# Input projection cut into columns of 512, 512, 260 and 260, with the halves of the squares added on GpSimd

## The chip, the cores and the metric

One core of a Trainium2 chip runs the whole kernel. The metric is the device time of one execution in microseconds (us), the median of several runs; lower is better.

## The reference

One layer of a streaming encoder, in fp32, with 2048 tokens of 1024 features and a memory of 256 tokens.

```python
# per layer (DEPTH = 1)
xn = rmsnorm(h, g_mix)
z = einsum('bsd,dc->bsc', xn, w_in)          # q | k | v (512 each), pool input (512), 8 forget logits
q, k = rmsnorm per head of 64
fox = forgetting_attention(q, k, v, f_logit) # causal softmax with cumulated log gates, 8 heads
pool = multiscale_pool(p_in)                 # trailing means over 2, 4, 8, 16 frames, linear map
h = h + concat(fox, pool) @ w_out
mn = rmsnorm(mem, g_mem_kv);  mkv = mn @ w_mem_kv
h = h + attention of rmsnorm(h) over the memory (4 heads of 128) @ w_mem_out
h = h + SwiGLU(rmsnorm(h))                   # 2816 hidden features
```

RMSNorm divides a token by the root of the mean of its squares. The part that concerns us is the first projection, `z`, and the two sums of squares it needs: those of the memory tokens and those of the tokens `x`.

## The kernel before

Every fp32 product is made from three products of split operands. `split` makes a high part (ScalarE casts to fp32r) and a low part (VectorE subtracts), and `mm3` issues high x high, high x low and low x high into the same PSUM bank (lines 65 to 70). So every logical matmul shows as three, on lines 68, 69 and 70.

**Order.** In the first part of the program (the `first` block) the instructions of TensorE, VectorE, ScalarE, GpSimd and the DMA queue of SyncE run exactly in the order in which they are written. An engine that waits holds up all that stands behind it in that order.

**The memory's keys and values.** For each of 8 slices `k` of 128 features, `split_kv(k)` splits the weights into the buffers `qs`, `kh`, `kl` in turn, and 12 matmuls of 512 columns go into four PSUM banks `kv`. Between the slices the loop has other work: squares of the memory tokens are collected (`x_split` with `mpart`), their sums and the reciprocal root are made at `k == 3` (`token_sums`, `token_rstd`), the first 256 tokens of `x` are split and squared at `k == 5` (`x_split(xt, part)`), and the projection's weights are split at `k == 6` and after the loop (`split_w_in`). `mpart` and `part` are the same single buffer, tag `part`.

**Squares and sums.** `x_split` loads tokens in four pieces of [128 features, 2 slices, 256 tokens]. ScalarE squares each; GpSimd adds the pieces 1 to 3 onto the first, so that `part` holds two halves of 256 tokens. `token_sums` adds over the features with TensorE: the squares are the stationary operand and a column of ones the moving one, for each half of the tokens (`j`) and each half of the squares (`c`) one matmul with a single column. `token_rstd` copies the sums out of PSUM with VectorE (line 213) and makes the reciprocal root with two small GpSimd operations (lines 77 and 79).

**The projection.** The 1544 columns of `w_qkvf` (q, k, v and 8 forget logits) are cut into four groups of `ZB = 386`. For each of 16 token tiles of 128 tokens, `project` runs 4 groups x 8 slices x 3 products = 96 matmuls into four PSUM banks `zps` (tag `z`, 4 buffers). In the first tile (`zps0`) the loop over slices is outside, since the weights are still being split; in the others the loop over groups is outside, and group 0 is followed by transposes of earlier heads (`to_heads`, line 402) and, in every second tile, by `token_sums` of the tile pair's squares. `scaled` evicts the four banks with ScalarE (line 350), multiplied by the token's reciprocal root. Then come the head norms (`normed_heads`, `gained_heads`, `head_parts`), and more transposes. The squares of the next block of 256 tokens are made a whole tile before they are summed.

After this stage come the projection of the pool input (`zp`), the pooling, the attention, the memory's attention and the SwiGLU stage, which the change does not touch.

Of the kernel before, what the change touches and what calls it, by code (L numbers as in the profile page):

```python
# [8 lines left out]
F32 = mybir.dt.float32  # L9
F32R = mybir.dt.float32r  # L10
AF = mybir.ActivationFunctionType
ALU = mybir.AluOpType
# [4 lines left out]
P = 128  # L17
S = 2048
D = 1024
KD = D // P  # L20
# [11 lines left out]
EPS = 1e-6  # L32
BIG = 3.0e38
QKVF = 3 * FOXW + H
ZB = QKVF // 4

# [2 lines left out]
def block_kernel(ctx: ExitStack, tc: tile.TileContext, x, xT, memT, cols, rows, w_qkvf, w_p, w_pool, w_out,  # L41
# [4 lines left out]
    act, dve, pool, pe, sp = nc.scalar, nc.vector, nc.gpsimd, nc.tensor, nc.sync  # L46

    def opened(stack, name, bufs=1, **kw):
        return stack.enter_context(tc.tile_pool(name=name, bufs=bufs, reuse_waits="tile", **kw))
# [12 lines left out]
    def sub_hi(lo, src, hi, eng=None):  # L62
        (eng or dve).tensor_tensor(out=lo, in0=src, in1=f(hi), op=ALU.subtract)  # L63

    def mm3(ps, st, mv, first, last, goes_on=False):

        (sh, sl), (mh, ml) = st, mv
        pe.matmul(ps, lhsT=sh, rhs=mh, start=first, stop=False, skip_group_check=goes_on)  # L68
        pe.matmul(ps, lhsT=sh, rhs=ml, start=False, stop=False, skip_group_check=goes_on)  # L69
        pe.matmul(ps, lhsT=sl, rhs=mh, start=False, stop=last, skip_group_check=goes_on)  # L70
# [22 lines left out]
    ones = cst.tile([P, P], F32, name="ones")  # L93
# [8 lines left out]
    def more_constants():  # L102
        dve.tensor_copy(identr[:], ident[:])

        dve.tensor_scalar(out=gqs[:, 0, :], in0=gqf, scalar1=-(DH ** -0.5), scalar2=None, op0=ALU.mult)
        dve.tensor_copy(gqs[:, 1, :], gkf)
        dve.tensor_scalar(out=gqm[:], in0=gq_mem, scalar1=P ** -0.5, scalar2=None, op0=ALU.mult)
    rstd = cst.tile([P, NT], F32, name="rstd")
# [16 lines left out]
    def slab(n, pl=None, dt=F32):  # L125
        n = ("qs", "kh", "kl", "cb")[n]
        return (pl or hpa).tile([P, S], dt, tag=n, name=n, bufs=1)
# [29 lines left out]
    def x_split(tiles, part=None, qs=range(4)):  # L157

        for q in qs:
            n, raw = tiles[q]  # L160
            hi = xp.tile([P, 2, B], F32R, tag="xhi", name="xhi", bufs=8)
            act.copy(hi[:], raw[:])
            if part is not None:
                sq = xp.tile([P, 2, B], F32, tag="xsq", name="xsq", bufs=2)[:] if q else part
                act.activation(sq, raw[:], AF.Square, scale=1.0 / 32.0)
                if q:
                    pool.tensor_tensor(out=part, in0=part, in1=sq, op=ALU.add)
            m, lo = xsl.take(F32R)
            sub_hi(lo[:], raw[:], hi[:])
            xsl.free.append(n)  # L170
            xlow.append(m)
            tiles[q] = hi, lo

    def x_part(tiles, k):
        return tuple(t_[:, k % 2] for t_ in tiles[k // 2])

    def x_parts(tiles):
        return tuple(zip(*(x_part(tiles, k) for k in range(KD))))
# [12 lines left out]
    whi = [None] * KD  # L191
    wlo = [None] * KD
# [4 lines left out]
    with ExitStack() as c0:  # L197
# [4 lines left out]
        def token_sums(part):  # L202

            ssp = tpp.tile([P, 2], F32, tag="ss", name="ss", bufs=1)
            for j in range(2):
                for c in range(2):
                    pe.matmul(ssp[:, j:j + 1], lhsT=part[:, c, j * P:(j + 1) * P], rhs=ones[:, 0:1], start=c == 0,
                              stop=c == 1)
            return ssp

        def token_rstd(ssp, outp):
            ms = xp.tile([P, 2], F32, tag="ms", name="ms", bufs=2)
            dve.tensor_copy(ms[:], ssp[:])
            rsqrt(outp, ms[:])
# [15 lines left out]
        def load_kv(k):  # L230
            wk[k] = w_in_hi(k, F32)[:, :2 * MW]
            sp.dma_start(wk[k], w_mem_kv[k * P:(k + 1) * P, :])

        def split_kv(k):
            t_ = slab(k % 3, dt=F32R)
            hi, lo = t_[:, :2 * MW], t_[:, 2 * MW:]

            w_ = MW if k == 0 else 2 * MW
            for c in range(0, 2 * MW, w_):
                split(hi[:, c:c + w_], lo[:, c:c + w_], wk[k][:, c:c + w_], g_mem_kv[:, k:k + 1])  # L240
            return hi, lo

        def load_w_in(k):

            n, raw = wsl.take(F32) if k < KD - 1 else (None, slab(3))
            w_raw[k] = n, raw[:, :QKVF]
            sp.dma_start(w_raw[k][1], w_qkvf[k * P:(k + 1) * P, :])

        def split_w_in(k):
            n, raw = w_raw[k]  # L250
            whi[k] = w_in_hi(k, F32R)
            wlo[k] = wsl.take(F32R)[1]
            split(whi[k][:], wlo[k][:], raw, g_mix[:, k:k + 1])
            wsl.free.append(n)
# [14 lines left out]
        for k in range(KD):  # L269
            if k == 0:  # L270
                raw = mt[0][1]
                x_split(mt, None, (0,))
            elif k < 4:
                x_split(mt, mpart[:], (k,))
            wh, wl = split_kv(k)
            if k == 0:
                act.activation(mpart[:], raw[:], AF.Square, scale=1.0 / 32.0)
            mh, ml = x_part(mt, k)
            if k == 3:
                token_rstd(token_sums(mpart), mr[:])  # L280
            for m in range(2):
                ms_ = slice(m * P, (m + 1) * P)
                for a in range(2):
                    as_ = slice(a * MW, (a + 1) * MW)
                    mm3(kv[m][a][:], (mh[:, ms_], ml[:, ms_]), (wh[:, as_], wl[:, as_]), k == 0, k == KD - 1)
            if k < 4:
                load_kv(k + 4)
            if k == 1:
                sp.dma_start(rowt[:], rows.partition_broadcast(P))
                load_w_in(0)  # L290
            if k == 3:
                for c in range(1, KD):
                    load_w_in(c)
            if k == 6:
                split_w_in(0)
            if k == 7:
                more_constants()
            if k == 5:
                part = xp.tile([P, 2, B], F32, tag="part", name="part", bufs=1)
                x_split(xt, part[:])  # L300
# [35 lines left out]
        with ExitStack() as c1:  # L336
            zpp = opened(xstack, "zpp", space=PSUM)

            def project(i, j, hs, ls, ns, k_outer=False):
                zps = {n: zpp.tile([P, ZB], F32, tag="z", name="zps", bufs=4) for n in ns}  # L340
                ts = slice(j * P, (j + 1) * P)
                for k, n in ([(k, n) for k in range(KD) for n in ns] if k_outer else [(k, n) for n in ns for k in range(KD)]):
                    sl = slice(n * ZB, (n + 1) * ZB)
                    mm3(zps[n][:], (hs[k][:, ts], ls[k][:, ts]), (whi[k][:, sl], wlo[k][:, sl]), k == 0, k == KD - 1)
                return zps

            def scaled(i, zps):
                z = slab(i % 2)
                for n in zps:
                    act.activation(z[:, n * ZB:(n + 1) * ZB], zps[n][:], AF.Copy, scale=rstd[:, i:i + 1])  # L350
                return z

            ssp = token_sums(part)
            for k in range(2, KD):
                split_w_in(k)
# [145 lines left out]
            for b in range(NB):  # L501
                hs, ls = x_parts(xt)
                for j in range(2):
                    i = 2 * b + j
# [8 lines left out]
                    if i == 0:  # L513
                        zps = zps0
                    else:
                        zps = project(i, j, hs, ls, range(1))
                        if i > 1:
                            to_heads(i - 2, zr, (3,))
                        else:
                            mem_keys()  # L520
                        if j == 0:
                            ssp = token_sums(part)
                        zps.update(project(i, j, hs, ls, range(1, 4)))
                        zr = split_heads(*st_)
                        if j == 0:
                            token_rstd(ssp, rstd[:, i:i + 2])
                    z = scaled(i, zps)
                    if i == NT - 3:
                        rb = stat_rows(stat_bcast(stat_diag(0)))
# [3 lines left out]
                    if j == 0:  # L533
                        if b + 1 < NB:
                            part = xp.tile([P, 2, B], F32, tag="part", name="part", bufs=1)
# [52 lines left out]
    with xstack:  # L588
# [66 lines left out]
        with in_order():  # L655
            mixed, mxs, pos, wop = {}, {}, {}, {}
            for n in range(NB + 3):
                if 0 < n < NB:
                    hs, ls = nxt
# [72 lines left out]
    with ExitStack() as c0:  # L732
# [228 lines left out]
        with in_order(EN.DVE, EN.Activation):  # L961
            sg, vg = all_scores(), all_values()
            lead, more = 0, True
            while True:
                if more and lead < LEAD:
                    n = next(sg, None)
                    more = n is not None
                    lead += more
                else:
                    n = next(vg, None)  # L970
# [136 lines left out]
    with ExitStack() as c0:  # L1107
# [138 lines left out]
        with in_order(EN.SP):  # L1246
# [14 lines left out]
            for n in range(NT + 1):  # L1261
# [6 lines left out]
                i = n + 2 if ahead else n + 1  # L1268
# [16 lines left out]
                i = n - 3  # L1285
# [10 lines left out]
                i = n - 1  # L1296
                if 0 <= i < NT:
                    pmd[i] = softmax(*qtd.pop(i), i >= NT - 3)
                i = n - 2
# [6 lines left out]
                i = n - 4  # L1306
# [314 lines left out]
```

## Time and profile before

| what | us |
|---|---|
| median of 3 runs | 2549.94 (2548.57 to 2550.21) |
| the profiled execution | 2547.98 |
| its span, first to last instruction | 2546.2 |
| TensorE busy in it | 2521.4 |
| VectorE, ScalarE, GpSimd busy | 1702.5, 1247.4, 777.8 |
| start (memory's keys and values), until the first projection | 0 to 34 |
| the input projection | 34 to 333 |

The profile is one execution. Rows of its timeline give the start and the duration of an instruction in us, the engine, the line of the kernel, the operation, out<-in by tile names, the shape, and in brackets the idle time of the engine before it and what ended it. PE is TensorE's matmul side, PEld its weight loads, DVE VectorE, ACT ScalarE, POOL GpSimd, SP SyncE. Matmuls overlap, so the distance between starts says what one costs.

### The profile page before, as it was taken

The page shows a single profiled execution, that of the slowest core. Times are in us where ns is not written, and L with a number is a line of the kernel's source. Part 1 is how long each engine was busy: PE and PEld are TensorE (multiplying, and loading weights), DVE is VectorE, ACT ScalarE, POOL GpSimd, SP SyncE. Part 2 cuts the span into 40 slices and gives each one's busy share as a digit, 9 for nine tenths or more (in the row PEclk, how much of TensorE's full clock was granted, in tenths as well). Part 3 has the DMA queues.
Part 4 walks back from the last instruction along what each step waited for, and adds up shares of the span by engine and source line. Part 5 has one row for each costly group of instructions (what it writes and reads, how often), then busy time and mean ns, then how long its engine had stood idle before and what let it go on. Part 6 is the DMA issues. An engine that isn't in the chain of part 4 may idle for free.

```text
span 2546.2 us, 36944 instructions
## 1 busy us (share of the span) xinstructions
PE 2521.4 (99%) x13155; PEld 2159.2 (85%) x13155; DVE 1702.5 (67%) x3018; ACT 1247.4 (49%) x2376; POOL 777.8 (31%) x1048
## 2 busy tenths in 40 slices
PE   9999999999999989999999999999999999999999
PEld 8999999878888878888878888888888888888887
DVE  7444386579999965545886877756766666665554
ACT  6454452169999945444544333334543333333443
POOL 3243210035554623333343544530001222222000
PEclk9999999999999999999999999999999999999999
DMA  6443375355554232212554554447672323324765
GB/s 250 125 132 109 116 240 157 134 162 144 125 149 133 86 121 75 87 72 87 204 214 168 184 190 162 180 167 274 237 262 101 126 99 109 123 100 173 239 207 204
DMA packets 204202, 396.20 MB, mean 156 GB/s; under 512 B 24305, under 2 KB 99825, under 8 KB 193265
## 3 DMA queue, kind: packets, MB, share of 16 engines
q1 hardware_dynamic: 174800, 297.35, 36.8%
q0 software_dynamic: 29216, 96.49, 9.8%
q8 instruction: 103, 1.69, 0.3%
q14 instruction: 83, 0.67, 0.1%
HBM read 268.85 MB, written 124.91 MB: 155 GB/s over the span
## 4 chain that ended last, share of the span: by engine, by line
PE 59%; DVE 2%; issue 1%; ACT 1%; POOL 0%; DMA 0%; POOLq 0%; DVEq 0%; ACTq 0%
PE bk L70 16%; PE bk L68 16%; PE bk L69 16%; PE mmps L68 3%; PE mmps L70 3%; PE mmps L69 3%; PE tp L985 1%; PE tp L1048 0%; DVE ww L63 0%; PE scps L70 0%; PE scps L69 0%; PE scps L68 0%; PE mops L70 0%; PE mops L69 0%; PE mops L68 0%
## 5 line engine op out<-in xcount | busy, mean ns | idle before, releaser
L63 DVE TENSOR_TENSOR ww<-draw,ww 128x512 fp32r<-128x512 f32 x308 | 204.3, 701 | 156.9 <-ACT ww L186 156.4
L186 ACT CAST ww<-draw 128x512 fp32r<-128x512 f32 x308 | 178.6, 620 | 220.7 <-PE bk L70 176.6
L63 DVE TENSOR_TENSOR ww<-graw,ww 128x512 fp32r<-128x512 f32 x220 | 175.1, 802 | 107.9 <-ACT ww L186 107.7
L69 PE MATMUL bk<-ww,ww 128*128 128x512 f32 x616 | 239.6, 389 | 0.0
L68 PE MATMUL bk<-ww,ww 128*128 128x512 f32 x616 | 239.6, 389 | 0.0
L70 PE MATMUL bk<-ww,ww 128*128 128x512 f32 x616 | 239.6, 389 | 0.0
L186 ACT CAST ww<-graw 128x512 fp32r<-128x512 f32 x220 | 135.8, 621 | 177.3 <-PE bk L70 160.0
L63 DVE TENSOR_TENSOR pl<-tp,ph 128x512 fp32r<-128x512 f32 (+3 forms) x298 | 177.3, 597 | 17.5 <-ACT ph L880 16.7
L68 PE MATMUL zps<-wh,xhi 128*128 128x386 f32 x512 | 175.7, 343 | 0.1
L69 PE MATMUL zps<-wl,xhi 128*128 128x386 f32 x512 | 173.5, 339 | 0.0
L70 PE MATMUL zps<-wh,xl 128*128 128x386 f32 x512 | 173.3, 339 | 0.0
L880 ACT CAST ph<-tp 128x512 fp32r<-128x512 f32 (+3 forms) x298 | 147.6, 514 | 15.1 <-PE tp L55 12.3
L70 PE MATMUL bk<-qs,ww 128*128 128x512 f32 x352 | 137.1, 390 | 1.1 <-DVE ww L63 1.1
L68 PE MATMUL bk<-qs,ww 128*128 128x512 f32 x352 | 137.9, 392 | 0.3 <-ACT s L1433 0.3
L69 PE MATMUL bk<-kh,ww 128*128 128x512 f32 x352 | 137.0, 389 | 0.0
L68 PE MATMUL bk<-kl,ww 128*128 128x512 f32 x352 | 136.9, 389 | 0.0
L69 PE MATMUL bk<-cb,ww 128*128 128x512 f32 x352 | 136.9, 389 | 0.0
L70 PE MATMUL bk<-kl,ww 128*128 128x512 f32 x352 | 136.9, 389 | 0.0
L70 PEld LDWEIGHTS bk<-ww,ww 128*128 128x128 f32 x616 | 115.6, 188 | 24.1
L69 PEld LDWEIGHTS bk<-ww,ww 128*128 128x128 f32 x616 | 115.7, 188 | 24.1
L68 PEld LDWEIGHTS bk<-ww,ww 128*128 128x128 f32 x616 | 115.7, 188 | 23.7
L1514 POOL DMA_DIRECT2D out_dram<-o x32 | 17.2, 540 | 382.6 <-DVE o L1511 376.8
(576 smaller groups left out, 7297.7 us busy)
## 6 DMA issues: line engine op xcount, KB each, us to landing
graw<-in_w_gu_dram SPq DMA_DIRECT2D x44, 1024.0 KB, 5.5
draw<-in_w_down_dram SPq DMA_DIRECT2D x66, 256.0 KB, 4.3
xl<-in_xT_dram SPq DMA_DIRECT2D x64, 256.0 KB, 4.6
qkT<-st SPq DMA_DIRECT2D x64, 256.0 KB, 2.7
wdr<-in_w_down_dram SPq DMA_DIRECT2D x22, 512.0 KB, 4.4
vd<-cb SPq DMA_DIRECT2D x16, 512.0 KB, 3.4
qs<-qkT SPq DMA_DIRECT2D x8, 1024.0 KB, 7.1
kh<-qkT SPq DMA_DIRECT2D x16, 512.0 KB, 9.7
```

The costliest lines, as they stand in the source:

```text
L63: (eng or dve).tensor_tensor(out=lo, in0=src, in1=f(hi), op=ALU.subtract)
L68: pe.matmul(ps, lhsT=sh, rhs=mh, start=first, stop=False, skip_group_check=goes_on)
L69: pe.matmul(ps, lhsT=sh, rhs=ml, start=False, stop=False, skip_group_check=goes_on)
L70: pe.matmul(ps, lhsT=sl, rhs=mh, start=False, stop=last, skip_group_check=goes_on)
L186: act.copy(hi, raw)
L880: act.copy(ph[:, sl], tp[:, sl])
L985: pe.transpose(tp[:, e_], src[:, q + e_], ident[:])
L1514: pool.dma_start(out[rows_, cs], o)
```

## The change

Three things change. The columns are cut at 0, 512, 1024, 1284 and 1544, so that two groups have 512 columns and two have 260; each PSUM tile is a bank of 512 columns of which a group uses its part. After the last piece of squares, GpSimd adds the second half of `part` onto the first (one addition of 128x256), and `token_sums` runs one matmul for each half of the tokens where it ran two. And the memory's sums and reciprocal root move from slice 3 to slice 5 of the memory's loop.

```diff
-ZB = QKVF // 4
+ZCUT = (0, 512, 1024, 1284, QKVF)
...
                 if q:
                     pool.tensor_tensor(out=part, in0=part, in1=sq, op=ALU.add)
+                if q == 3:
+                    pool.tensor_tensor(out=part[:, 0], in0=part[:, 0], in1=part[:, 1], op=ALU.add)
...
             for j in range(2):
-                for c in range(2):
-                    pe.matmul(ssp[:, j:j + 1], lhsT=part[:, c, j * P:(j + 1) * P], rhs=ones[:, 0:1], start=c == 0,
-                              stop=c == 1)
+                pe.matmul(ssp[:, j:j + 1], lhsT=part[:, 0, j * P:(j + 1) * P], rhs=ones[:, 0:1], start=True, stop=True)
             return ssp
...
             mh, ml = x_part(mt, k)
-            if k == 3:
+            if k == 5:
                 token_rstd(token_sums(mpart), mr[:])
...
             def project(i, j, hs, ls, ns, k_outer=False):
-                zps = {n: zpp.tile([P, ZB], F32, tag="z", name="zps", bufs=4) for n in ns}
+                zps = {n: zpp.tile([P, 512], F32, tag="z", name="zps", bufs=4)[:, :ZCUT[n + 1] - ZCUT[n]] for n in ns}
...
-                    sl = slice(n * ZB, (n + 1) * ZB)
-                    mm3(zps[n][:], (hs[k][:, ts], ls[k][:, ts]), (whi[k][:, sl], wlo[k][:, sl]), k == 0, k == KD - 1)
+                    sl = slice(ZCUT[n], ZCUT[n + 1])
+                    mm3(zps[n], (hs[k][:, ts], ls[k][:, ts]), (whi[k][:, sl], wlo[k][:, sl]), k == 0, k == KD - 1)
...
                 for n in zps:
-                    act.activation(z[:, n * ZB:(n + 1) * ZB], zps[n][:], AF.Copy, scale=rstd[:, i:i + 1])
+                    act.activation(z[:, ZCUT[n]:ZCUT[n + 1]], zps[n], AF.Copy, scale=rstd[:, i:i + 1])
```

In the order of the instructions on each engine nothing else moves: behind the projection the two programs issue the same instructions in the same order.

## The prediction

> **What bounds the kernel now.** I read the page first: span, then the busy time of TensorE (PE).
>
> ```profile
> span 2546.2 us, 36944 instructions
> PE 2521.4 (99%) x13155; PEld 2159.2 (85%) x13155; DVE 1702.5 (67%) x3018; ACT 1247.4 (49%) x2376; POOL 777.8 (31%) x1048
> ```
>
> PE is busy for 99% of the span, so what the change takes from PE comes off the end, unless it opens a wait there. Next I read busy time by stage. The input projection of tokens 128 to 2047 lies in 51 to 333 us; columns are length, then busy us and instructions of PE, weight loads, VectorE (DVE), ScalarE (ACT), GpSimd (POOL), then granted clock, DMA share and GB/s.
>
> ```profile
> 51.00:333.00 282.00, 282.00 (x1734) 280.87 (x1733) 125.56 (x140) 134.36 (x232) 101.97 (x68) 1.00 0.39 118
> ```
>
> PE has no idle time there at full clock, and no other engine is busy half of it. In this stage a matmul costs the distance from its start to the next start, not its recorded duration (0.34 us for 386 columns, of which half overlaps the next one). Those distances come from the timeline of PE.
>
> ```profile
> 155.27 0.34 PE L68 MATMUL zps<-wh,xhi 128*128 128x386 f32 x1
> ...
> 163.56 0.34 PE L70 MATMUL zps<-wh,xl 128*128 128x386 f32 x1
> ...
> 335.13 0.28 PE L68 MATMUL zp<-xhi,wph 128*128 128x256 f32 x1
> ...
> 344.49 0.28 PE L70 MATMUL zp<-xhi,wpl 128*128 128x256 f32 x1
> ...
> 950.88 0.28 PE L68 MATMUL scps<-ww,ww 128*128 128x256 f32 x1
> ...
> 952.20 0.28 PE L70 MATMUL scps<-ww,ww 128*128 128x256 f32 x1
> ...
> 2199.84 0.39 PE L68 MATMUL bk<-kl,ww 128*128 128x512 f32 x1
> ...
> 2203.46 0.39 PE L69 MATMUL bk<-s4l,ww 128*128 128x512 f32 x1
> ```
>
> Each pair is the first and last start of an unbroken run. 386 columns: 48 matmuls, 47 steps in 8.29 us, 176.4 ns a step. 256 columns: 80 steps in 9.36 us, 117.0 ns; in another stage 11 steps in 1.32 us, 120 ns. 512 columns: 16 steps in 3.62 us, 226.3 ns.
>
> **Part 1, the cut of the 1544 columns.** A token tile has 96 matmuls (4 groups, 8 slices of features, 3 products). Before, all have 386 columns; after, 48 have 512 and 48 have 260. No row has 260 columns. The line from 256 to 512 has (226.3 - 117.0) / 256 = 0.427 ns a column, so four more columns add 1.7 ns: 118.7 from the lower row, 121.7 from the upper. I take 120. For 512 I take 227, between 226.3 and 228 (an estimate that allows for the slower steps after a switch). Twice in each tile PE returns from 128-column transposes, and the first step is longer:
>
> ```profile
> 163.73 1.14 PE L402 MATMUL tp<-identr,kl 128*128 128x128 f32 x12
> 164.71 0.41 PE L68 MATMUL zps<-wh,xhi 128*128 128x386 f32 x1
> 164.96 0.34 PE L69 MATMUL zps<-wl,xhi 128*128 128x386 f32 x1
> ...
> 1507.12 0.60 PE L1048 MATMUL bk<-ident,h 128*128 128x128 f32 x4
> 1507.47 0.47 PE L68 MATMUL bk<-qs,ww 128*128 128x512 f32 x1
> 1507.79 0.39 PE L69 MATMUL bk<-kh,ww 128*128 128x512 f32 x1
> ```
>
> It takes 0.25 us with 386 columns and 0.32 us with 512; after the change both returns fall on groups of 512. Before: 2 x 0.25 + 94 x 0.1764 = 17.08 us a tile. After: 2 x (0.32 + 23 x 0.227) + 48 x 0.120 = 16.84. That is 0.24 less in each of 15 tiles; the first tile has no return inside it: 96 x 0.1764 - 48 x (0.227 + 0.120) = 0.28. Sum: **-3.9 us**. With 118.7 and 226.3 it is 0.33 a tile, -5.3; with 121.7 and 228 it is 0.11, -1.8.
>
> The Trainium skill, "TensorE: Matmul & The Clock Gate", section "Back-to-back issue gap", gives the warm gap as columns / 2.4 + 2.5 ns. By that rule any cut into four costs the same and this term would be 0. The trace differs: 176.4 ns for 386 where the rule has 163.3, and 226.3 for 512 where it has 215.8, so the fixed part is not one number here. I go by the rows, and keep the rule's outcome as a rival.
>
> ScalarE evicts the four groups with other widths (about as much in sum: 1544 columns either way). Cover: the next tile needs the first bank again at 164.71, as quoted.
>
> ```profile
> 159.35 1.53 ACT L350 ACTIVATE qs<-zps,rstd 128x386 f32<-128x386 f32 x3 [2.47 <-POOL rstd L79]
> ```
>
> The first eviction ends at about 159.35 + 0.51 = 159.9; at 512/386 of its length it would end 0.17 later, against 4.8 us of slack. I cost it at nothing; without that cover it would be 0.17 us a tile, 2.7 in all.
>
> **Part 2, the sums over features.** `token_sums` runs four matmuls with one column, which the trace shows as eight.
>
> ```profile
> 150.06 1.02 PE L207 MATMUL ss<-ones,part 128*128 128x1 f32 x8
> 150.94 0.43 PE L68 MATMUL zps<-wh,xhi 128*128 128x386 f32 x1
> ...
> 135.21 5.75 POOL L167 TENSOR_TENSOR part<-part,xsq 128x512 f32<-128x512 f32 x3
> ```
>
> Eight take 0.88 us, 0.11 each; four go away: 0.44. It happens once for each of 8 blocks of tokens: **-3.5 us** (the call for the memory is in part 3). GpSimd pays with an addition of 128x256: no row has it; between 0.96 us (half of 5.75 / 3) and 1.92. GpSimd's additions end at 140.96, 9.1 us before the sums read them, so the new one is hidden.
>
> **Part 3, the start: the memory's sums move from slice 3 to slice 5.** This is where I expect the money to go. In program order the step on DVE (`ms` from PSUM, L213) now stands behind the low parts of slices 4 and 5 and in front of the four subtractions for the first tokens; on PE it stands behind all matmuls of slice 4. No DMA is issued by the step, and SP's order stays.
>
> ```profile
> 17.86 0.16 DVE L213 COPY ms<-ss 128x2 f32<-128x2 f32 x1 [0.83 <-PE ss L207]
> 19.16 1.28 DVE L182 SCALAR_TENSOR_TENSOR kl<-wh,colt,kl 128x1024 fp32r<-128x1024 f32 x1
> 20.36 4.89 DVE L63 TENSOR_TENSOR xl<-xl,xhi 128x512 fp32r<-128x512 f32 x4
> 25.18 2.32 DVE L182 SCALAR_TENSOR_TENSOR qs<-wh,colt,qs 128x1024 fp32r<-128x1024 f32 x1
> ...
> 19.54 0.63 ACT L165 ACTIVATE part<-xl 128x512 f32<-128x512 f32 x1
> ...
> 18.12 1.21 POOL L77 TENSOR_SCALAR ms<-ms 128x2 f32<-128x2 f32 x1 [2.83 <-DVE ms L213]
> 19.41 1.63 POOL L79 TENSOR_TENSOR mr<-ms,mhalf 128x2 f32<-128x2 f32 x1
> 21.29 5.13 POOL L167 TENSOR_TENSOR part<-part,xsq 128x512 f32<-128x512 f32 x3 [0.25 <-ACT xsq L165]
> ...
> 23.37 0.40 PE L68 MATMUL kv<-kl,xhi 128*128 128x512 f32 x1
> 27.55 0.50 PE L69 MATMUL kv<-qs,xhi 128*128 128x512 f32 x1 [0.98 <-DVE qs L182]
> 33.16 0.95 PE L207 MATMUL ss<-ones,part 128*128 128x1 f32 x8
> 33.97 0.42 PE L68 MATMUL zps<-wh,xhi 128*128 128x386 f32 x1
> ```
>
> Slice 5 starts on PE at 23.37; without the 0.88 us of sums at slice 3 it would be about 22.5. There the sums run now, and DVE gets its copy at about 23.1. DVE is free from 20.4 and waits 2.7 us, with the subtractions and slice 6 queued behind it. ACT waits as well: `part` has one buffer, so its write at 19.54 waits until PE has read the memory's squares, and the cast of slice 6 is queued behind. GpSimd comes after DVE: its two small operations (1.21 + 1.63) now precede the three additions, which start at about 25 to 26 instead of 21.29 and end at 30 to 31. In the trace, DVE's low part of slice 6 took 2.32 us where that of slice 5 took 1.28: it went through only when GpSimd's additions had ended (21.29 + 5.13 = 26.42). So it ends at 31 to 32.9 instead of 27.50, and PE waits for it: at 27.55 it already waited 0.98 us for this very instruction. The new addition of about 0.7 to 1 us falls in the same place, and one earlier ahead of slice 3's low part. From this the first projection, 33.97 now, starts 2.5 us later at least (DVE's wait alone, less some catching up) and 6 at most (5.4 from slice 6, one addition of 1, less 0.44 for the sums at 33.16). I take **+5**, near the upper end, since slice 6 did wait for the additions before.
>
> With PE almost idle from about 26 to 31.6 the clock may fall. The trace has such a fall in the attention stage:
>
> ```profile
> 897.06:900.47 3.41, 0.97 (x5) 0.39 (x4) 1.69 (x3) 2.80 (x5) 0.84 (x1) 1.00 0.00 2
> 900.48:903.89 3.41, 1.83 (x8) 1.65 (x9) 3.41 (x8) 3.41 (x9) 1.91 (x3) 0.50 0.02 5
> 903.89:907.30 3.41, 3.41 (x20) 3.11 (x19) 3.10 (x5) 2.62 (x6) 2.18 (x3) 0.50 0.00 0
> ```
>
> PE was busy 0.97 of 3.41 us, then the granted clock was 0.50 for 6.8 us. After a wait of 5 us, 3.4 to 5 us of PE's work would run at half clock, 1.7 to 2.5 us lost, of which about 1 falls into the wait for slice 7. I take **+1.2**, with 0 (no fall) and 2.5 as ends. The Trainium skill has this on the same page, section "What's actually happening": a gate with two states, moved by windows of 3413 ns. The trace agrees: 6.8 us is two of them.
>
> **Sum** on the profiled execution: 2547.98 (span 2546.2 and 1.8 around it) - 3.9 - 3.5 + 5.0 + 1.2 = 2546.8. The median of the runs, 2549.94, is 1.96 above that execution, so I forecast **2548.7**, 1.2 below it. A measurement of this kernel can tell about 0.2%, 5.1 us, from no change: the forecast is no change.
>
> **The rivals.** *Little or no stall* (0.25): if DVE and ACT catch up and GpSimd does not hold them, the start costs 2.5 and the clock stays: -4.9, 2545.0; with no stall at all -7.4, 2542.5. For it: DMA-fed casts leave ACT some slack. Against it: the copy stands in DVE's order as said, and PE already waited there. I give 0.15 of the 0.25 to times below 2544.8.
>
> *One price by columns* (0.12): if a step is a fixed part plus a part by columns, the cut brings 0 and the rest +2.7: 2552.6. For it: 260, like 386, is no power of two, and may carry the 3.9 ns by which 386 lies above the line (117.0 + 130 x 0.427 = 172.5); then the term is about -1.1. The Trainium skill's rule named in part 1 gives the same time.
>
> *Slower: weight loads* (0.13). Every matmul has a load of its own weights, and the short groups leave less time to hide it:
>
> ```profile
> L70 PEld LDWEIGHTS zps<-wh,xl x512: 187/188/192, 34.2 to 332.7; 128*128 128x128 f32 x171
> ```
>
> A load is recorded with 188 ns (the middle number). If loads paced PE at that, 768 matmuls (16 tiles x 48) of 260 columns would cost 68 ns more each than the 120 of part 1: +52, 2601. It decides from 128 ns on: 768 x 8 ns = 6.1, 2554.9, about 0.2% above. Against it: the 386 columns of this very line already step at 176.4, below 188, so loads overlap each other, and 256 columns stream at 117 and 120.
>
> **Numbers.** Forecast 0.50, little stall 0.25, one price 0.12, slower 0.13. The bounds of all terms together give -6.3 to +3.2, that is 2543.6 to 2553.1; the range 2543.0 to 2553.0 takes in 2545.0 and 2552.6 and leaves out 2542.5 and all beyond 2554.9. Faster by over 0.2%: 0.15; slower: 0.13; within: 0.72.
>
> **What would show it.** In the profile after: steps of 227 and 120 ns in `zps`; four `ss` instructions a call; DVE's copy `ms` at about 23 us waiting for PE `ss`; the wait of PE for slice 6 grown from 0.98 to some 4 us; the first `zps` at about 39 instead of 33.97; a granted clock of 0.50 near 30 us. The forecast is wrong if the first `zps` starts before 36.5, or if 260 columns take under 117 or over 126 ns.

## The result and the profile after

The changed kernel takes 2553.53 us (median; 2551.18 to 2556.03), the kernel before, run beside it, 2550.07. The ratio is 1.0013, with a 95% interval of 1.0007 to 1.0019: slower by 3.3 us, less than the 0.2% named in the prediction, and 0.5 above the upper end of its range. The profiled execution took 2551.99, 4.01 more than that of before.

The first lines of the page after:

```profile
span 2550.3 us, 36881 instructions
PE 2520.0 (99%) x13119; PEld 2122.3 (83%) x13119; DVE 1703.4 (67%) x3018; ACT 1249.3 (49%) x2376; POOL 793.4 (31%) x1057
```

TensorE has 36 matmuls fewer (18 written ones, each shown as two) and GpSimd nine additions more. Two stretches follow, with the columns of the prediction's row: the projection stage, and the start around the late slice 6.

```profile
51.00:333.00 282.00, 282.00 (x1725) 248.80 (x1724) 129.44 (x145) 136.22 (x233) 115.82 (x78) 1.00 0.39 118
26.00:34.00 8.00, 3.78 (x11) 2.47 (x10) 7.91 (x5) 6.45 (x7) 5.50 (x4) 0.84 1.01 418
```

The projection stage is still TensorE without a gap at full clock. At the start TensorE is busy 3.78 of 8 us, and the granted clock is 0.84 on average. The timeline of PE after shows the start and then one token tile:

```profile
23.07 0.50 PE L208 MATMUL ss<-ones,part 128*128 128x1 f32 x4
...
28.51 0.49 PE L68 MATMUL kv<-qs,xhi 128*128 128x512 f32 x1 [2.03 <-ACT qs L183]
31.20 0.63 PE L69 MATMUL kv<-qs,xhi 128*128 128x512 f32 x1 [2.19 <-DVE qs L184]
...
34.18 0.63 PE L70 MATMUL kv<-qs,xl 128*128 128x512 f32 x1
...
38.21 0.50 PE L208 MATMUL ss<-ones,part 128*128 128x1 f32 x4
38.58 0.48 PE L68 MATMUL zps<-wh,xhi 128*128 128x512 f32 x1
...
39.94 0.50 PE L68 MATMUL zps<-wh,xhi 128*128 128x512 f32 x1 [0.42 <-DVE qs L184]
...
149.27 0.47 PE L68 MATMUL zps<-wh,xhi 128*128 128x512 f32 x1
149.58 0.40 PE L69 MATMUL zps<-wl,xhi 128*128 128x512 f32 x1
...
155.95 0.39 PE L69 MATMUL zps<-wl,xhi 128*128 128x512 f32 x1
...
161.06 0.39 PE L70 MATMUL zps<-wh,xl 128*128 128x512 f32 x1
161.29 0.28 PE L68 MATMUL zps<-wh,xhi 128*128 128x260 f32 x1
...
166.95 0.29 PE L70 MATMUL zps<-wh,xl 128*128 128x260 f32 x1
```

Read it in three places. Slice 6 waits 2.03 us for the high part of its weights (ScalarE) and then 2.19 for the low part (VectorE), and the first projection starts at 38.58 instead of 33.97. Each call of the sums has four instructions. And the steps: from 155.95 to 161.06 lie 22 steps of 512 columns, **232.3 ns** each; from 161.29 to 166.95, 47 steps of 260, **120.4 ns**. What holds up slice 6 is on the other engines:

```profile
23.60 0.16 DVE L213 COPY ms<-ss 128x2 f32<-128x2 f32 x1 [2.86 <-PE ss L208]
23.71 0.69 DVE L63 TENSOR_TENSOR xl<-xl,xhi 128x512 fp32r<-128x512 f32 x1
...
25.88 3.06 DVE L63 TENSOR_TENSOR xl<-xl,xhi 128x512 fp32r<-128x512 f32 x2 [0.35 <-ACT xhi L162]
28.86 2.29 DVE L184 SCALAR_TENSOR_TENSOR qs<-wh,colt,qs 128x1024 fp32r<-128x1024 f32 x1
...
23.66 0.63 ACT L165 ACTIVATE part<-xl 128x512 f32<-128x512 f32 x1 [3.74 <-PE ss L208]
...
23.86 0.65 POOL L77 TENSOR_SCALAR ms<-ms 128x2 f32<-128x2 f32 x1 [7.40 <-DVE ms L213]
24.59 0.73 POOL L79 TENSOR_TENSOR mr<-ms,mhalf 128x2 f32<-128x2 f32 x1
25.41 4.64 POOL L167 TENSOR_TENSOR part<-part,xsq 128x512 f32<-128x512 f32 x3
30.14 1.60 POOL L169 TENSOR_TENSOR part<-part 128x256 f32<-128x256 f32 x1
```

The copy stands still until the sums at 23.07 are done. GpSimd's additions then run from 25.41 to 31.74, and VectorE's low part of slice 6 (L184 `qs`) ends at 31.15, where PE's wait ends.

Cut at the first `zps` and the first `zp`, the profiled executions compare as follows, with two experiments beside them.

| us | before | after | cut and sums, memory's sums at slice 3 | move alone |
|---|---|---|---|---|
| start to the first `zps` | 33.97 | 38.58 | 33.74 | 39.28 |
| first `zps` to first `zp` | 300.74 | 297.25 | 297.25 | 300.74 |
| first `zp` to the end | 2211.54 | 2214.46 | 2214.54 | 2212.09 |
| span | 2546.24 | 2550.29 | 2545.52 | 2552.11 |

After against before: +4.61 at the start, -3.49 in the projection, +2.92 behind it.

### The profile page after: what moved, and what is told of

The parts are those of the page before. It is cut to its first block, busy times and chain, and to the rows that moved or that the text cites. A ratio compares the mean times of both kernels' runs of the same rounds, so it can differ in the third digit from the quotient of the medians.

```text
span 2550.3 us, 36881 instructions
## 1 busy us (share of the span) xinstructions
PE 2520.0 (99%) x13119; PEld 2122.3 (83%) x13119; DVE 1703.4 (67%) x3018; ACT 1249.3 (49%) x2376; POOL 793.4 (31%) x1057
## 3 DMA queue, kind: packets, MB, share of 16 engines
q8 instruction: 103, 1.69, 0.3%
## 4 chain that ended last, share of the span: by engine, by line
PE 51%; issue 8%; DVE 2%; ACT 1%; POOL 1%; DMA 0%; SPq 0%; POOLq 0%; DVEq 0%; ACTq 0%
PE bk L70 13%; PE bk L69 13%; PE bk L68 13%; PE mmps L68 3%; PE mmps L70 3%; PE mmps L69 3%; PE tp L985 1%; DVE ww L63 0%; DMA xraw<-hTd 0%; ACT pm L1182 0%; POOL out_dram L1514 0%; PE tp L1048 0%; PE scps L70 0%; PE scps L69 0%; PE scps L68 0%
## 5 line engine op out<-in xcount | busy, mean ns | idle before, releaser
L68 PE MATMUL zps<-wh,xhi 128*128 128x260 f32 (+1 forms) x512 | 175.5, 343 | 0.4 <-DVE qs L184 0.4
L69 PE MATMUL zps<-wl,xhi 128*128 128x260 f32 (+1 forms) x512 | 173.5, 339 | 0.0
L70 PE MATMUL zps<-wh,xl 128*128 128x260 f32 (+1 forms) x512 | 173.3, 338 | 0.0
```

## The experiments

**The start back at slice 3.** `e1_sums_at_3`: the changed kernel with

```diff
-            if k == 5:
+            if k == 3:
                 token_rstd(token_sums(mpart), mr[:])
```

> The changed kernel with one thing undone: the memory's sums stand at slice 3 again. Theory 'stall': the move alone opened the wait at the start, so the first projection starts at about 34.1 us instead of 38.6, the granted clock does not fall, the projection stage stays as in the changed kernel (297.2 us from first zps to first zp), and the time is 3 to 4 us below the kernel before. Rival 'late cost': the 2.9 us that the changed kernel lost behind the projection come from the cut or the sums themselves; then they stay, and the time is within 1 us of the kernel before.

Measured: 2547.76 (ratio 0.9992, 0.9983 to 1.0002); run a second time as `e12_sums_at_3_again` 2547.24 (0.9987, 0.9977 to 0.9996). In the timeline of PE of the first of these runs the projection starts as early as before, and the time that the sums save is given back one group of columns later:

```profile
33.74 0.48 PE L68 MATMUL zps<-wh,xhi 128*128 128x512 f32 x1
...
35.10 0.50 PE L68 MATMUL zps<-wh,xhi 128*128 128x512 f32 x1 [0.42 <-DVE qs L184]
```

What follows: the move is what makes the change slower; cut and sums without it are 2.9 and 3.1 us faster than before by the medians, and only the second run's interval leaves out 1. The late cost that the rival names stays, though: 2214.54 us behind the projection. So the gain came at the lower edge of the 3 to 4 us that the theory gave.

**The cut alone.** `e2_cut_only`: the kernel before with `ZCUT` for `ZB` in `project` and `scaled`, as in the change's diff.

> The kernel before with the new cut of the columns alone. Theory 'one price by columns': 512 columns cost 232 ns a step and 260 cost 120.5 in this stage, so the stage from first zps to first zp is 300.7 - 0.6 + 0.3 = 300.4 us, and the time is within 0.5 us of the kernel before. Rival, the prediction's step: with the sums and the stall out of the way 512 columns step at 227 ns and the time is 3.9 us lower. Rival 'late cost': 2 to 3 us slower with an unchanged stage.

Measured: 2550.27 (1.0001, 0.9992 to 1.0009). The projection stage takes 299.89 instead of 300.74: 0.22 less in the first tile and 0.04 less in each of 15. The cut is worth 0.85 us: more than the 0.3 of the theory, and far from the 3.9 of its rival.

**The sums alone.** `e3_sums_only_at_3`: the kernel before with

```diff
+                if q == 3:
+                    pool.tensor_tensor(out=part[:, 0], in0=part[:, 0], in1=part[:, 1], op=ALU.add)
...
-                for c in range(2):
-                    pe.matmul(ssp[:, j:j + 1], lhsT=part[:, c, j * P:(j + 1) * P], rhs=ones[:, 0:1], start=c == 0,
-                              stop=c == 1)
+                pe.matmul(ssp[:, j:j + 1], lhsT=part[:, 0, j * P:(j + 1) * P], rhs=ones[:, 0:1], start=True, stop=True)
```

> The kernel before with the addition on GpSimd and the halved sums alone, the memory's sums still at slice 3, groups of 386 columns. Theory: 7 calls in the projection stage save 0.43 us each, 3.0, the start stays within 0.3 us of 33.97, so the time is 3 us below the kernel before. Rival: GpSimd's addition holds VectorE up in the stage and takes part of it back; then the stage from first zps to first zp is longer than 298.2 us.

Measured: 2549.15 (0.9993, 0.9985 to 1.0002). The projection stage is 298.06: 7 blocks of tokens give 0.447 each, 3.13, and the first tile loses 0.45. The stage is as the theory has it, the median is not: 1.5 us under that of before instead of 3, and not clear of noise. In this execution the first `zps` started late, at 36.02, since the slices were late and the clock fell for 3.4 us from 29.86. The added additions alone don't do that: with them and the sums at slice 3, `e1_sums_at_3` starts at 33.74 and `e12_sums_at_3_again` at 33.89.

**The move alone.** `e4_move_only`: the kernel before with

```diff
-            if k == 3:
+            if k == 5:
                 token_rstd(token_sums(mpart), mr[:])
```

> The kernel before with the memory's sums moved from slice 3 to slice 5 alone. Theory 'stall': the first zps starts 3.5 to 5 us later than 33.97, with a wait for slice 6 and a granted clock of 0.5 near 31 us, and the time is 3.5 to 5 us above the kernel before. Rival: the new addition on GpSimd makes most of the stall; then the first zps starts less than 2.5 us later.

Measured: 2554.09 (1.0014, 1.0005 to 1.0023), as much slower as the whole change. The timeline of PE:

```profile
31.15 0.79 PE L69 MATMUL kv<-qs,xhi 128*128 128x512 f32 x1 [1.91 <-DVE qs L182]
...
39.28 0.42 PE L68 MATMUL zps<-wh,xhi 128*128 128x386 f32 x1
```

Slice 6 goes on at 31.15, as in the changed kernel, and the projection starts 5.3 us late. The clock was 0.50 here for 6.8 us from 28.4; in the changed kernel's profiled execution for 3.4. The new addition on GpSimd is not in this kernel, so the rival is out.

**Which of the queues holds slice 6 up.** Two edits of the changed kernel. `e5_own_buffer` gives the memory's squares a buffer of their own, so that ScalarE need not wait for PE:

```diff
-        mpart = xp.tile([P, 2, B], F32, tag="part", name="part", bufs=1)
+        mpart = zp.tile([P, 4, P], F32, tag="st", name="mpart", bufs=4)[:].rearrange("p a c -> p (a c)").rearrange("p (a t) -> p a t", a=2)
```

> The changed kernel, but the memory's squares have a buffer of their own, so ScalarE's first write of the next squares no longer waits for TensorE's sums. Theory 'VectorE and GpSimd hold the start': VectorE's copy still stands before the four subtractions, and GpSimd's reciprocal root still before its additions, which ScalarE's fourth square waits for; the first zps moves by less than 1 us from 38.6. Rival 'ScalarE's buffer wait holds the start': then the first zps falls to about 35 us.

`e6_copy_later` does this too and leaves the sums at slice 5 on PE, but issues VectorE's copy and GpSimd's root two slices later:

```diff
             if k == 5:
-                token_rstd(token_sums(mpart), mr[:])
+                ssm = token_sums(mpart)
...
             if k == 7:
+                token_rstd(ssm, mr[:])
```

> As the run with a buffer of its own, and the copy of the sums on VectorE with the reciprocal root on GpSimd stands behind slice 7; TensorE's sums stay at slice 5. Theory: nothing waits at the start any more, the first zps comes at 33.7 us (as with the sums at slice 3) within 0.5, no fall of the clock before 100 us, and the time is 3 us below the kernel before. Rival: the place of the sums on TensorE itself makes the stall; then the first zps stays above 37 us.

Measured: 2553.33 (1.0011, 1.0002 to 1.0020) and 2550.98 (1.0003, 0.9994 to 1.0012). The timelines of ScalarE and VectorE with the own buffer:

```profile
19.04 0.63 ACT L165 ACTIVATE part<-xl 128x512 f32<-128x512 f32 x1
...
27.14 0.63 ACT L165 ACTIVATE xsq<-xl 128x512 f32<-128x512 f32 x1 [4.88 <-POOL part L167]
...
28.84 2.37 DVE L184 SCALAR_TENSOR_TENSOR qs<-wh,colt,qs 128x1024 fp32r<-128x1024 f32 x1 [1.19 <-ACT qs L183]
```

ScalarE writes `part` at 19.04 instead of 23.66, and gains nothing: it then waits until 27.14 for GpSimd, whose additions still stand behind the root. The first `zps` comes at 39.17, no earlier than in the changed kernel. With the copy late, the timelines of PE and ScalarE read:

```profile
28.20 0.50 PE L69 MATMUL kv<-qs,xhi 128*128 128x512 f32 x1 [1.23 <-DVE qs L184]
...
35.13 0.50 PE L68 MATMUL zps<-wh,xhi 128*128 128x512 f32 x1 [0.34 <-ACT mks L310]
...
34.39 0.69 ACT L310 ACTIVATE mks<-kv,mr 128x512 f32<-128x512 f32 x1 [5.04 <-POOL mr L79]
```

Slice 6 is nearly on time (28.20; before 27.55). So it was the place of the copy and the root in VectorE's and GpSimd's order; the buffer alone changes nothing. Whether the shared buffer would still hold slice 6 with a late copy was not run. I had expected the projection at 33.7 and no fall of the clock; it came at 35.13, since the root is now late and the eviction of the memory's keys and values waits for it, and the clock fell for 3.4 us from 38.3, which left the projection stage at 299.95 us. One wait went and another took its place.

**The clock.** `e7_fill`: the changed kernel with 28 matmuls into an unused bank ahead of slice 6, in PE's idle time:

```diff
+            if k == 6:
+                fill = tpp.tile([P, B], F32, tag="tp", name="fill", bufs=3)
+                for n in range(28):
+                    pe.matmul(fill[:], lhsT=x_part(mt, 5)[0][:, :P], rhs=x_part(mt, 5)[0], start=True, stop=True)
```

> The changed kernel with 28 matmuls of 256 columns added on TensorE ahead of slice 6, where it waits; their results are not used. Theory 'the fall of the clock has a price of its own': TensorE stays busy until 29.4, the granted clock stays 1.00 at 31 us, the wait for slice 6 still ends at 31.2, and the first zps comes about 1 us earlier than 38.6; over the runs the mean granted clock returns to that of the kernel before (0.998) and the median falls by 1 to 2 us against the changed kernel. Rival: the fall lies wholly inside the wait; then the first zps stays at 38.6 within 0.3 us and the time does not change.

Measured: 2550.21 (1.0001, 0.9992 to 1.0010). The same stretch as above, 26 to 34 us:

```profile
26.00:34.00 8.00, 6.80 (x44) 5.82 (x42) 7.91 (x5) 6.45 (x7) 5.56 (x4) 1.00 1.02 420
```

PE is busy 6.80 of 8 us and the clock stays at 1.00. The stall is the same (slice 6 goes on at 31.26), and the first `zps` comes at 37.70, 0.88 earlier than in the changed kernel. That is the 1 us of the theory. The median is 3.3 lower, more than the 1 to 2 expected; the 28 matmuls also put back most of the 36 that were taken out, which matters below.

**The stretch behind the projection.** The two programs issue the same instructions there, yet of the kernels told so far those with the new sums took 2214.5 to 2215.5, and the others 2211.5 to 2213.1. The clearest place is a load. Timelines of ScalarE, of before and then of after, at the cast of a piece of the memory's output weights:

```profile
984.58 0.63 ACT L186 CAST wm21h<-wmr 128x512 fp32r<-128x512 f32 x1
```

```profile
987.04 0.62 ACT L188 CAST wm21h<-wmr 128x512 fp32r<-128x512 f32 x1 [0.86 <-DMA wmr<-in_w_mem_out_dram]
```

After, the load lands later; through VectorE and GpSimd that reaches PE, whose timelines of before and of after read:

```profile
988.50 0.63 PE L985 MATMUL tp<-ident,mq 128*128 128x128 f32 x4 [0.18 <-POOL pm L1185]
```

```profile
990.96 0.63 PE L985 MATMUL tp<-ident,mq 128*128 128x128 f32 x4 [1.06 <-POOL pm L1185]
```

The page has a queue that the kernel does not issue:

```profile
q8 instruction: 103, 1.69, 0.3%
```

These are 103 packets of 16 KB. 1.69 MB over TensorE's 13119 matmuls and 13119 loads is about 64 bytes each, which the Trainium skill, "Perfetto Trace Analysis", section "The 4-stage abstract model", gives as the size of an instruction: so this is probably TensorE's program. In the packet records of before, one of them starts at 641.2 us after the first `zp`, in front of the load of `wm21h`; after, the same one by order starts at 648.2, inside that load. It runs from 984.04 to 985.46, the load from its issue at 983.50 to its landing at 986.94: 3.44 us where it took 2.56 before. That taking 36 matmuls and their loads out ahead moves every later block back by as many instructions is my reading of this. Five runs bear on it. `e8_before_again` is the kernel before once more.

> The kernel before once more, for a second trace. Theory 'the 2.9 us behind the projection are spread from run to run': the stretch from first zp to the end, 2211.5 us in the first trace, comes out elsewhere between 2211 and 2215. Rival 'the change costs 2.9 us behind the projection': it is 2211.5 again within 0.5.

`e10_half_sums` is the kernel before with one matmul for each half of the tokens, and no addition: the second half of the squares is left out of the sums.

```diff
-                for c in range(2):
-                    pe.matmul(ssp[:, j:j + 1], lhsT=part[:, c, j * P:(j + 1) * P], rhs=ones[:, 0:1], start=c == 0,
-                              stop=c == 1)
+                pe.matmul(ssp[:, j:j + 1], lhsT=part[:, 0, j * P:(j + 1) * P], rhs=ones[:, 0:1], start=True, stop=True)
```

> The kernel before with one matmul for each half of the tokens in token_sums and no addition on GpSimd: the second half of the squares is left out of the sums. TensorE has 36 matmuls fewer, all other engines have the same instructions as before. Theory of the fetch: the projection stage is 3.1 to 3.5 shorter (297.3), the fetch near 641 us after the first zp falls at 647 to 649, the cast of wm21h waits about 1 us for its load, and the stretch from the first zp to the end is 2214.5 instead of 2211.5 to 2212.1: the run gains about 1, 2548 to 2549.5. Rival (GpSimd's additions do it): the stretch stays at 2212 and the run gains 3.5, 2546.5.

`e9_same_count` (with the memory's sums at slice 3) and `e11_after_same_count` (as changed, slice 5) put the number of matmuls back in the warm-up:

```diff
-        for n in range(22):
-            pe.matmul(wps[:], lhsT=warm[:, :P], rhs=warm[:, :B], start=True, stop=True)
+        for n in range(58):
+            w_ = B if n < 8 else 64
+            pe.matmul(wps[:, :w_], lhsT=warm[:, :P], rhs=warm[:, :w_], start=True, stop=True)
```

> The changed kernel with the memory's sums back at slice 3, and with as many TensorE instructions as the kernel before: the 22 warm-up matmuls ahead of the first slice become 58 shorter ones (8 of 256 columns and 50 of 64), which puts back the 36 matmuls that the new sums took out. Theory (TensorE fetches its own instructions in blocks of 16 KB, and with 36 matmuls fewer the blocks after the projection fall 6 to 10 us later, one of them onto the load of the memory's output weights): the fetch near 641 us after the first zp returns to 641, ScalarE's cast of wm21h no longer waits for its load, the stretch from the first zp to the end goes from 2214.5 back to 2212, and the median is about 2.4 under that of the same kernel without the fill, 2545. Rival (the nine additions on GpSimd, or the other widths of eviction, do it): the stretch stays at 2214.5 and the median at 2547.8.

> The changed kernel as it is, with the memory's sums at slice 5, and the same fill of the warm-up. Theory of the fetch: the first zps stays at 38.6 (39.3 if the clock falls for two windows), the stretch from the first zp to the end goes from 2214.5 to 2212, the median from 2553.5 to about 2551. Rival: the stretch stays at 2214.5 and the median at 2553.5.

> The changed kernel with the memory's sums at slice 3 once more, as the neighbour of the filled one on the same chip. Both theories: the median near 2547.8, the stretch from the first zp to the end near 2214.5, the fetch 6 us late.

Measured, with what the trace shows of each (us; "wait" is ScalarE's at `wm21h`, the fetch is counted from the first `zp`, "second fall" is how long the clock fell once more, at 910 to 916 us from the start, behind the fall near 900):

| | median | ratio (95%) | fetch | wait | first `zp` to end | SwiGLU stage | second fall |
|---|---|---|---|---|---|---|---|
| `e8_before_again` | 2548.49 (one run) | | 641.1 | none | 2212.05 | 1268.54 | none |
| `e11_after_same_count` | 2558.03 | 1.0032 (1.0019 to 1.0044) | 641.9 | none | 2212.34 | 1268.49 | none |
| `e9_same_count` | 2554.36 | 1.0016 (1.0007 to 1.0025) | 645.2 | none | 2215.00 | 1268.55 | 6.8 |
| `e10_half_sums` | 2549.60 | 0.9995 (0.9986 to 1.0004) | 649.5 | 0.44 | 2216.84 | 1269.46 | 3.4 |
| `e12_sums_at_3_again` | 2547.24 | 0.9987 (0.9977 to 0.9996) | 650.1 | 0.63 | 2216.38 | 1268.54 | 3.4 |
| after | 2553.53 | 1.0013 (1.0007 to 1.0019) | 648.2 | 0.86 | 2214.46 | 1269.07 | none |

The warm-up was a mistake of mine: 58 short matmuls were to take as long as 22 long ones, and took 7.9 us more, so the medians of the two filled kernels tell nothing. This is the first line of PE's timeline of `e9_same_count`, and then the same line of before:

```profile
2.04 12.59 PE L262 MATMUL warm<-cb 128*128 128x256 f32 x58 [2.04 <-POOL cb L258]
```

```profile
2.04 4.71 PE L261 MATMUL warm<-cb 128*128 128x256 f32 x22 [2.04 <-POOL cb L258]
```

Their late stretches do tell something. Over all 14 executions with a trace: the seven with 36 matmuls fewer all wait 0.3 to 1.0 us for that load, and the seven others at most 0.1. The SwiGLU stage takes 1269.07 to 1269.63 in six of those seven (1268.54 in the other), and 1268.49 to 1268.61 in all seven others. A third place goes the same way. In all of the seven, and in none of the others, PE waits 0.25 to 0.28 us for GpSimd near 896 us after the first `zp`; PE's timelines of before and of after read there:

```profile
1229.61 0.63 PE L985 MATMUL tp<-ident,mq 128*128 128x128 f32 x4
```

```profile
1232.46 0.63 PE L985 MATMUL tp<-ident,mq 128*128 128x128 f32 x4 [0.28 <-POOL hr L79]
```

`e10_half_sums` shows all three without any addition on GpSimd, and `e11_after_same_count` loses all three and is back at 2212.34. So the number of TensorE's instructions does it, not GpSimd's work. That the fetch is the way is shown by its timing at the load alone; at the two other places it isn't shown.

Several numbers came out otherwise than expected. `e9_same_count` was to return to 2212 and took 2215.00, with the fetch at 645.2; its clock fell a second time, for 6.8 us, nearly 70 us ahead of that fetch, and PE is 2.7 us later from there on. `e10_half_sums` and `e12_sums_at_3_again`, each with a second fall of 3.4 us that costs 1.5, are above the 2214.5 expected mostly for the same reason. `e8_before_again` is 0.51 from the first trace, at the edge of its rival: the 2.92 are more than those two traces of one kernel differ. The second fall came in six of 14 executions, one of them with as many matmuls as before. The changed kernel's profiled execution has none, so it is no part of its 2.92.

Set start by start against the first trace of before, the 2.92 us of the changed kernel are 0.43 near 18 us after the first `zp`, 0.87 at the load, 0.39 near 892 to 896, 0.65 near 912 and 0.58 in the SwiGLU stage. Those at the load, near 892 to 896 and in the SwiGLU stage go with the missing matmuls: 1.84 in all. The 0.65 near 912 is in the second trace of before too (0.81), as is a shift near 18 us (0.32, the other way): these two are spread between executions.

## Why the prediction was right and wrong

It forecast -1.2 for the profiled execution, and +4.01 was measured. Two steps failed, by about 3 us each: the cut, and the stretch behind the projection. By its own steps (us):

| step | forecast | measured | from |
|---|---|---|---|
| part 1, the cut | -3.9 | -0.85 | the cut alone |
| part 2, eight sums at 0.44 | -3.5 | -3.1 | seven at 0.447; the first is given back |
| part 3, start and clock | +5.0 +1.2 | +5.1 | +4.61, with 0.44 put back for the first sums |
| behind the projection | 0 | +2.9 | first `zp` to end |

Given back is the first block's saving: PE is 0.44 earlier at the first `zps` and then waits 0.42 at 39.94 for VectorE, which evicts the memory's values; the first tile is longer by 0.45.

**The first step that failed is the 227 ns for 512 columns in part 1.** I took it from the SwiGLU stage (226.3). The trace of before had 512 columns at another pace as well, in the memory's projection, in front of the very stage that is cut:

```profile
14.54 0.40 PE L70 MATMUL kv<-kl,xl 128*128 128x512 f32 x1
...
16.65 0.39 PE L70 MATMUL kv<-kl,xl 128*128 128x512 f32 x1
```

Nine steps in 2.11 us are 234.4 ns. Measured in `zps`: 232.3. The 260 columns came as forecast (120.4 against 120), and so did the first step after the transposes (0.31 against 0.32). The 5.3 ns by which 512 columns are slower are 48 x 5.3 = 254 ns a tile, all of the 0.24 us that the cut was to bring. The three widths in `zps` (120.4, 176.4, 232.3) lie on one line: 112 ns over 252 columns is 0.444 ns a column, and 120.4 - 260 x 0.444 leaves 5.0 ns a matmul; 386 columns come to 176.4 by it. This is the rival "one price by columns". The Trainium skill's section "Back-to-back issue gap" in "TensorE: Matmul & The Clock Gate" has that form and was right in it, though not in its figures (111, 163 and 216 ns by it).

**The stall was right in its place and nearly in its size.** The copy came at 23.60 (said: about 23) waiting for PE's sums, PE waited 4.2 us for slice 6 (about 4), the first `zps` came at 38.58 (about 39), and the clock fell at 31.4 (near 30). The rival "little or no stall" is out. One reading under it was wrong: that VectorE's low part of slice 6 goes through only when GpSimd's additions have ended. After, it ended at 31.15, before the last addition (31.74); it took 2.29 us beside the additions where slice 5's took 1.28, so they slow it and don't hold it. That the forecast end of 31 to 32.9 came true is in part luck. `part` and its single buffer, which I also named, is not what has to be undone: with its own buffer the stall stays.

**The clock was sized for one execution, and varies.** In the profiled execution it fell once, for 3.4 us, and cost 0.88 (against the filled kernel), within my 0 to 2.5 and under the 1.2 that I took; with the move alone it fell for 6.8. Over all runs the mean granted clock is 0.9971 after and 0.9984 in the filled kernel, so the profiled execution, at 0.998, was among the mild ones. The kernel with the fill is 3.3 below the changed one; how much of that is the clock and how much the matmuls put back isn't separated.

**The parts do not add up by the medians.** The move alone cost 3.5 us, the cut and the sums without it gained 2.9 and 3.1, and together they cost 3.5. Each of the ratios of the experiments has an interval of about 0.09% (2.3 us) either way, which leaves room for this; it isn't settled. The table above goes by single executions, and that of before was a quick one: 2547.98 against a median of 2550.07.

**The second step that failed is the zero behind the projection.** "Nothing else moves" was true of the order and not of the time. I counted that stretch at nothing, since its instructions are the same, and it took 2.92 us more. Of these, 1.84 came at three places where only executions with 36 matmuls fewer lose time; the rest is spread between executions. At one of the places a block of the program met a load that was waited for.

The rival that loads of weights would pace the 260 columns is out: 120.4 ns, under the 128 from which it would have decided.

## What to carry to other kernels

Take the price of a matmul from the stage nearest to the one you change, and look for a second row of the same shape before you trust the first; here 2.3% in one price (227 against 232.3 ns) was the whole gain. A small step that is moved "later" in engines that run in order moves everything queued behind it, and what it costs is read from who waits for that queue, then from the clock that falls in the gap. The better version undoes only the move: memory's sums at slice 3 with the new cut and sums, 2547.2 to 2547.8 against 2550.3 to 2550.6 before.

## What the runs showed of the hardware

Blocks of TensorE's own program travel among the kernel's loads (103 packets of 16 KB), and with 36 matmuls and 36 weight loads fewer, those behind the first `zp` came 0.7 to 14.4 us later, counted from it and matched by order.

A matmul at the very start cost 0.217 us on average with 50 of 58 at 64 columns (12.59 / 58), and 0.214 with 256 columns (4.71 / 22): there, its width did not matter. Why isn't shown. The narrow ones did not bring the full clock either: in `e9_same_count` TensorE runs them from 2.04 to 14.4 us without a gap, and the matmuls of 512 columns behind them still step at 427 ns up to 18.0 us and at 230 to 238 from 18.4 on, while before the steps of 256 columns fall from 213 to 117 ns near 6.2 us.

512 columns take 226.3 ns a step in the SwiGLU stage and 232.3 in the projection, both without a gap. These are the paces of stages and not of single rows: the median step is 227 ns in `bk`, `mmps` and `oo`, 233 in `kv` (before) and 232 in `zps` (after). No run here explains it.

VectorE's subtraction of 128x512 took 0.69 us at 23.71, and 1.53 (3.06 / 2) at 25.88 while GpSimd added two inputs. The Trainium skill, "GPSIMD Engine Reference", section "1. Specifications", says that GpSimd shares its SBUF interfaces with VectorE, with contention where VectorE has two SBUF inputs; the trace agrees, and here it costs the factor 2.2.
